# Block products for the Fourier chunks too, a new order of the seven products, and two conditioning groups on TensorE

## The chip, the cores and the metric

The kernel runs on one core of a Trainium2 chip. The metric is the device time of one execution in microseconds, as the median of several runs. A profile is one execution taken by the hardware profiler; its span is the time from the first to the last instruction. Engines: PE is TensorE (matmuls; PEld its weight loads), DVE is VectorE, ACT is ScalarE, POOL is GpSimd, SP issues most of the transfers.

## The reference

Two layers, one after the other, work on 640 tokens (512 latent and 128 context tokens) of width 1024. Of each layer, cut to what matters here:

```python
shift, scale, gate = _modulation(cond, w_mod[l], b_mod[l])        # silu(cond) @ w_mod + b_mod
h = _layernorm(x) * (1.0 + scale) + shift
q, k, v, z_a, cb, cc, cx, z_b, fx, z_c, g = jnp.split(h @ w_in[l], offsets, axis=-1)
y_a = attn_fn(q, k, v) * silu(z_a)
y_b = _short_conv(cb, cc, cx, conv_w[l]) * silu(z_b)
y_c = _fourier(fx) * silu(z_c)          # real part of a 2-D DFT over positions and 128 channels
gates = sigmoid(g.reshape(b, s, 3, 1024))
merged = gates[:, :, 0] * (y_a @ w_branch[l, 0]) + gates[:, :, 1] * (y_b @ w_branch[l, 1]) \
       + gates[:, :, 2] * (y_c @ w_branch[l, 2])
x = _layernorm(ALPHA * x + gate * (merged @ w_o[l])) * ln_g[l] + ln_b[l]
```

## The kernel before

Activations lie with channels on the 128 partitions and the 640 tokens along the free axis. A float32 product is made of three float32r products: each operand is split into a high part (a ScalarE copy) and a low part (a VectorE subtraction), and high·high, high·low and low·high are summed in PSUM. The activations h lie split in the tile `act`.

The input projection of a layer is 58 chunks of 128 columns: Q 4, K 1, V 1, ZA 4, CB, CC, CX and ZB 4 each (the convolution), FX 4 and ZC 4 (the Fourier branch), and 24 of gates. A **plain chunk** (`inproj`, L505 to L507) takes eight k steps of six matmuls (three of 256 and three of 384 tokens), with two split weight buffers `hlw`, one for each half. A **pair** (`pair`, L957) makes two gate chunks at once: it cuts the 2x2 blocks of input halves and chunks so that seven products of 12 matmuls with 320 columns are enough where eight are due. It needs sums of blocks of the activations (tiles `tb` and `tf`, made by `sums(0)`, `sums(1)` and `last_sum` in the Fourier stage) and of the weights (the `Sum` steps), and each product adds to one of three PSUM banks `y`, `x`, `z`, from which ScalarE copies (`keep`) and VectorE adds (`plus`) gather the gate tiles (`ga` for branch 0, `gs` for the others).

The stages of a layer are: LayerNorm and Q, K, V; attention, with the plain ZA and convolution chunks as fillers between its units; the Fourier stage, which alternates plain FX and ZC chunks with `channels(g)` (the DFT over channels) and `positions(g)` (over positions) of four groups; the gate stage, twelve pairs in the order of branches 1, 2, 0, each pair of branch 1 and 2 followed by its two branch products (`pb`); and the output product with the closing LayerNorm.

The program is a list of jobs. `run()` walks through it and puts the weight loads (at most N_RAW = 6 raw buffers) and their splits (at most N_HL = 5 split buffers `hl`) as far ahead of the products as these buffers allow. A scheduler then fixes one order for each engine; on the chip an engine works its list in that order and waits on semaphores. The scratch tiles `tmp` share three buffers: `channels` takes two for its results `ah` and `al`, and the conditioning work takes others.

Conditioning (scale, shift and gate from `w_mod`) comes in groups (l, n). Those of layer 0 that the first LayerNorm needs are made by TensorE at the start (`mod_rows`, L459, and `mod_columns`, L468). The others are made by VectorE: an accumulator `moda` takes 16 operations a group over loads `rawm` (L236 and L239), then a transpose, a reduction and a small matmul. Groups (0,4), (0,5) and (1,0) run as `mod_steps` beside layer 0's attention, the others as `mod_piece`, one after each pair: twelve pieces in layer 0 and eight in layer 1.

## Time and profile before

| | |
|---|---|
| time, median of 3 runs | 1243.19 us (1242.01 to 1244.68) |
| profiled execution of before | 1243.65 us, span 1241.9 us, mean granted clock 0.996 |
| busy: PE, DVE, ACT, POOL | 1211.6, 918.7, 568.3, 182.1 us |
| moved by DMA | 137.38 MB, mean 111 GB/s |

The profiled execution is 1.75 us longer than its span; that part lies outside the instructions. Busy times of the engines overlap, so they don't add up to the span: an engine with a share near 100% sets the pace, and another one matters where it makes that engine wait. A matmul's duration in a row includes its way through the array; how fast matmuls follow one another is read from the starts.

### The profile page before, as it was taken

What the parts mean: (1) busy time and instruction counts of PE and PEld (TensorE: products, weight loads), DVE (VectorE), ACT (ScalarE), POOL (GpSimd) and SP (SyncE); (2) the same over time, 40 slices, a digit from 0 to 9 for tenths busy, and PEclk for the clock granted to TensorE, in tenths of its full rate; (3) what the DMA queues carried; (4) which work ended last, traced back from release to release, by engine and by line L of the source; (5) the groups of instructions that cost most, each with busy time, mean ns of one, the idle gap of its engine ahead of it and who ended that gap; (6) DMA issues with size and microseconds to landing.
All of it is one profiled execution on the core that took longest, in us unless ns stands there. A gap on an engine that the chain in (4) does not pass through costs nothing.

```text
span 1241.9 us, 20937 instructions
## 1 busy us (share of the span) xinstructions
PE 1211.6 (98%) x8016; PEld 1166.8 (94%) x8016; DVE 918.7 (74%) x1683; ACT 568.3 (46%) x1100; POOL 182.1 (15%) x180
## 2 busy tenths in 40 slices
PE   5999999999999999999999999999999999999997
PEld 4899999999999999999889999999999999999986
DVE  5795697879799876677888665666869966666766
ACT  4345636456344344463245646545444344445300
POOL 2003424041000000000230324232000000000001
PEclk8999999999999999999999999999999999999999
DMA  9632131313255452453412211112223533433351
GB/s 353 235 113 69 52 119 60 102 60 120 62 160 153 128 151 71 102 174 135 158 72 82 73 56 60 51 55 93 92 57 125 160 111 92 131 88 106 105 187 51
DMA packets 64085, 137.38 MB, mean 111 GB/s; under 512 B 7600, under 2 KB 8176, under 8 KB 63728
## 3 DMA queue, kind: packets, MB, share of 16 engines
q1 hardware_dynamic: 59232, 125.35, 30.5%
q0 software_dynamic: 4176, 10.39, 4.1%
q8 instruction: 63, 1.03, 0.4%
q10 hardware_dynamic: 576, 0.30, 0.1%
q14 instruction: 38, 0.31, 0.1%
HBM read 130.48 MB, written 5.52 MB: 110 GB/s over the span
## 4 chain that ended last, share of the span: by engine, by line
PE 88%; DVE 6%; DMA 2%; issue 2%; ACT 1%; POOL 1%; DVEq 0%; SPq 0%; POOLq 0%
PE y L957 13%; PE p L505 12%; PE p L507 12%; PE p L506 12%; PE z L957 6%; PE pb L505 4%; PE pb L507 4%; PE pb L506 4%; PE x L957 3%; PE pt L694 2%; PE s L645 2%; PE p L422 2%; PE o L1118 2%; PE o L1117 2%; PE o L1119 2%
## 5 line engine op out<-in xcount | busy, mean ns | idle before, releaser
L505 PE MATMUL p<-act,hlw 128*128 128x256 f32 (+1 forms) x1024 | 321.0, 314 | 0.9 <-ACT qr L69 0.9
L507 PE MATMUL p<-act,hlw 128*128 128x256 f32 (+1 forms) x1024 | 318.9, 311 | 0.0
L506 PE MATMUL p<-act,hlw 128*128 128x256 f32 (+1 forms) x1024 | 317.4, 310 | 0.0
L505 PEld LDWEIGHTS p<-act,hlw 128*128 128x128 f32 x1024 | 193.3, 189 | 2.8 <-ACT qr L69 1.2
L506 PEld LDWEIGHTS p<-act,hlw 128*128 128x128 f32 x1024 | 192.8, 188 | 1.5
L507 PEld LDWEIGHTS p<-act,hlw 128*128 128x128 f32 x1024 | 192.8, 188 | 1.3
L676 POOL TENSOR_SCALAR P<-P,rc 128x384 f32<-128x384 f32 (+2 forms) x80 | 115.5, 1459 | 233.2 <-ACT hlw L69 101.4
L69 ACT ACTIVATE hlw<-raww 128x512 fp32r<-128x512 f32 x136 | 85.2, 629 | 109.0 <-PE p L507 97.0
L147 DVE TENSOR_TENSOR hlw<-raww,hlw 128x512 fp32r<-128x512 f32 x134 | 92.4, 693 | 25.0 <-ACT hlw L69 23.9
L1117 PE MATMUL o<-wo,act 128*128 128x512 f32 (+1 forms) x168 | 63.8, 381 | 0.0
L1118 PE MATMUL o<-wo,act 128*128 128x512 f32 (+1 forms) x168 | 63.5, 379 | 0.0
L1119 PE MATMUL o<-wo,act 128*128 128x512 f32 (+1 forms) x168 | 63.1, 379 | 0.0
L72 DVE TENSOR_TENSOR pT<-pt,pT 128x512 fp32r<-128x512 f32 x60 | 40.1, 685 | 20.9 <-ACT pT L69 20.8
L69 ACT ACTIVATE gs<-y 128x320 f32<-128x320 f32 x48 | 20.8, 433 | 67.3 <-PE y L957 66.3
L239 DVE SCALAR_TENSOR_TENSOR moda<-rawm,scond,moda 128x512 f32<-128x512 f32 x70 | 51.0, 742 | 0.0
L69 ACT ACTIVATE pT<-pt 128x512 fp32r<-128x512 f32 x60 | 34.9, 592 | 31.5 <-PE pt L694 25.0
L648 DVE CUSTOM_DVE_ANT_0 P<-s,mask 128x384 f32<-128x384 f32 (+1 forms) x64 | 38.5, 617 | 10.3 <-PE s L645 10.2
L670 ACT ACTIVATE P<-P,nm 128x384 f32<-128x384 f32 (+1 forms) x64 | 42.1, 658 | 1.2 <-DVE es L72 0.7
L75 DVE TENSOR_TENSOR gs<-pb,gs 128x640 f32<-128x640 f32 x16 | 13.2, 825 | 38.6 <-PE pb L507 38.6
L505 PE MATMUL pb<-ya,hlb 128*128 128x256 f32 (+1 forms) x128 | 40.1, 313 | 0.1
L505 PE MATMUL pb<-yc,hlb 128*128 128x256 f32 (+1 forms) x128 | 39.9, 311 | 0.0
L505 PE MATMUL pb<-yb,hlb 128*128 128x256 f32 (+1 forms) x128 | 39.8, 311 | 0.0
(722 smaller groups left out, 2888.5 us busy)
## 6 DMA issues: line engine op xcount, KB each, us to landing
raww<-in_w_in SPq DMA_DIRECT2D x136, 256.0 KB, 2.9
rawm<-in_w_mod SPq DMA_DIRECT2D x36, 512.0 KB, 4.3
rawg<-in_w_in SPq DMA_DIRECT2D x72, 256.0 KB, 3.4
rawb<-in_w_branch SPq DMA_DIRECT2D x48, 256.0 KB, 3.1
rawo<-in_w_o SPq DMA_DIRECT2D x32, 256.0 KB, 3.0
sz<-in_w_mod SPq DMA_DIRECT2D x24, 256.0 KB, 3.0
dft<-in_dft POOLq DMA_DIRECT2D x2, 1542.0 KB, 7.6
x<-in_x SPq DMA_DIRECT2D x5, 512.0 KB, 8.3
```

The costliest lines, as they stand in the source:

```text
L69: nc.scalar.activation(out, in_, AF.Copy)
L147: eng.tensor_tensor(out=self.hl[:, 1], in0=raw, in1=fr(self.hl[:, 0]), op=ALU.subtract)
L239: nc.vector.scalar_tensor_tensor(out=acc[:, c], in0=w, scalar=scond[:, k, c:c + 1], in1=acc[:, c], op0=ALU.mult, op1=ALU.add)
L505: nc.tensor.matmul(ps[:, a:b], lhsT=ld.w(0, k), rhs=mh, start=k == 0, stop=False)
L506: nc.tensor.matmul(ps[:, a:b], lhsT=ld.w(0, k), rhs=ml, start=False, stop=False)
L507: nc.tensor.matmul(ps[:, a:b], lhsT=ld.w(1, k), rhs=mh, start=False, stop=k == nk - 1)
L670: nc.scalar.activation(P[:, g, :W], srcs[g], AF.Exp, scale=0.125, bias=nm_[:, g:g + 1], accum_out=sm[:, g:g + 1])
L676: nc.gpsimd.tensor_scalar(out=P[:, g, :W], in0=P[:, g, :W], scalar1=rc[:, g:g + 1], scalar2=None, op0=ALU.mult)
L957: nc.tensor.matmul(out, lhsT=ld.w(z, k), rhs=moving(k, y), start=first and k == i == 0, stop=k == 3 and i == 2, skip_group_check=True)
L1117: nc.tensor.matmul(ps, lhsT=act[:, t, 0, k], rhs=w[:, 0], start=k == 0, stop=False)
L1118: nc.tensor.matmul(ps, lhsT=act[:, t, 0, k], rhs=w[:, 1], start=False, stop=False)
L1119: nc.tensor.matmul(ps, lhsT=act[:, t, 1, k], rhs=w[:, 0], start=False, stop=k == NK - 1)
```

## The change

FX and ZC chunks become four pairs per layer, named f{l}0, f{l}2 (FX) and f{l}4, f{l}6 (ZC); their results lie in a tile `fz`. The convolution and ZA chunks stay plain. The block sums move into the attention (`aside` and `last_sum`). The seven products of every pair come in another order of banks, with the weight steps in the order that goes with it. Groups (0,4) and (0,5) are made by TensorE in layer 0's attention (`mod_group`), from loads into tiles of the tags T and F; group (1,0) becomes four more pieces of layer 0's gate stage, sixteen in all, and a pair of branch 2 is followed by two pieces. yb and ya stay unsplit in the attention, and `split_y` splits them in the gate stage. Tiles of SBUF change their tags accordingly, and so do the loads of w_o.

```diff
-        side = mod_steps(((0, 4), (0, 5), (1, 0)) if l == 0 else (), lambda: S["moda"], lambda: S["modr"])
+        if l == 0:
+            aside = {0: [groups[0][1]], 1: [groups[0][2], groups[1][1]], 2: [groups[1][2]]}
+        else:
+            aside = {}
+        aside.update({3: [begin_sums, sums(0)], 6: [sums(1)]})
...
+    def mod_group(l, n, tag):
...
+        def rows():
+            pr = aux(f"modp{l}{n}")
+            for k in range(NK):
+                c = 32 * (k % 4)
+                nc.tensor.matmul(pr[c:c + 32], lhsT=scond32[:, k], rhs=w["raw"][:, k * 512:(k + 1) * 512],
+                                 start=k < 4, stop=k >= 4, tile_position=(0, c))
+            w["rows"] = row(f"modr{l}{n}")[:, 0:512]
+            copy(w["rows"], pr)
+
+        def columns():
+            ps = aux(f"modq{l}{n}")
+            for i in range(4):
+                nc.tensor.matmul(ps[:, 2 * i:2 * i + 2], lhsT=w["rows"][:, i * 128:(i + 1) * 128], rhs=pick,
+                                 start=True, stop=True)
...
-            for i in range(2):
-                mod_add(mod_acc[l, n], 2 * kp + i, mod_raw[p][:, i * 512:(i + 1) * 512])
+            with tc.issue_after(last["gate"].ins):
+                mod_add(mod_acc[l, n], 2 * kp, mod_raw[p][:, 0:512])
+            mod_add(mod_acc[l, n], 2 * kp + 1, mod_raw[p][:, 512:1024])
...
-            job(seventh("y", old(0, 0), True, keep(0, 0)), Load([s1, a11, a12, a22], [hl(a11, [], 1)]))
-            job(seventh("x", old(0, 1), True, plus(0, 0)), Load([], [hl(a12, [], 2)]))
-            job(seventh("z", new(0), True, lambda out: None), Load([], [hl(s1, [], 5), Sum(add, s1, s1, a11)]))
...
-            job(seventh("y", new(1), False, keep(0, 1)), Load([], [hl(s1, [], 6), Sum(sub, a11, s1, a22), Sum(add, a12, a12, s1, [s1])]))
-            job(seventh("y", new(2), False, third_y), Load([], [hl(a11, [a11], 7)]))
-            job(seventh("y", lambda k, z: act[:, :, z, k, 64:128], False, last_y), Load([], [hl(a22, [a22], 4)]))
...
-            job(seventh("z", old(1, 1), False, last_z), Load([], [hl(a12, [a12], 3)]))
+                self.steps = [
+                    (Load([s1, a11, a12, a22], [hl(a11, [], 1)]), "y", old(0, 0), self.keep(0, 0)),
+                    (Load([], [hl(s1, [], 5)]), "z", new(0), self.keep(1, 1)),
+                    (Load([], [Sum(add, s1, s1, a11), hl(s1, [], 6)]), "y", new(1), self.keep(0, 1)),
+                    (Load([], [hl(a12, [], 2)]), "x", old(0, 1), self.plus(0, 0)),
+                    (Load([], [Sum(sub, a11, s1, a22), Sum(add, a12, a12, s1, [s1]), hl(a11, [a11], 7)]), "y", new(2),
+                     self.plus(1, 1)),
+                    (Load([], [hl(a12, [a12], 3)]), "z", old(1, 1), self.last_z),
+                    (Load([], [hl(a22, [a22], 4)]), "y", lambda k, z: act[:, :, z, k, 64:128], self.last_y)]
...
-        inproj(l, C_FX, use_fx(0))
...
-        for g in range(4):
-            job(channels(g))
-            inproj(l, C_ZC + g, use_zc(g))
...
+        p = fourier_pair(C_FX, 0, use_fx)
+        p.emit()
+        p = fourier_pair(C_ZC, 4, use_zc)
+        p.emit(4)
+        job(channels(0))
+        p.emit(2)
+        job(channels(1))
+        p.emit(1)
+        p = fourier_pair(C_FX, 2, use_fx)
+        p.emit(2)
+        job(positions(0))
+        p.emit(3)
+        job(positions(1))
+        p.emit(2)
+        p = fourier_pair(C_ZC, 6, use_zc)
+        p.emit(3)
+        job(channels(2))
+        p.emit(2)
+        job(channels(3))
+        p.emit(2)
+        job(positions(2))
+        job(positions(3))
+
+        pieces = [(1, n, kp) for n in (range(4) if l == 0 else (4, 5)) for kp in range(4)]
...
+                if (b, m) == (1, 0):
+                    job(split_y("yb", "C"))
                 piece()
+                if b == 2:
+                    piece()
+                if (b, m) == (0, 1):
+                    job(split_y("ya", "A"))
+                if (b, m) in ((0, 2), (0, 3)):
+                    load_wo(1, "D", m - 2)
```

On TensorE, at the start of layer 0's gate stage, the list of before reads as follows (`hlg010p` are the split weights of branch 1's first pair, `hlg011p` of its second; what stands ahead of the arrow is the bank):

```order
L957 MATMUL y_3753<-act,hlg010p_3503 128x320 x12
L957 MATMUL x_3774<-act,hlg010p_3583 128x320 x12
L957 MATMUL z_3793<-tb_3030,hlg010p_3586 128x320 x12
L957 MATMUL y_3753<-tb_3030,hlg010p_3697 128x320 x12
L957 MATMUL y_3893<-act,hlg011p_3806 128x320 x2
L957 MATMUL x_3914<-act,hlg011p_3822 128x320 x2
L957 MATMUL y_3753<-tf_3031,hlg010p_3704 128x320 x12
L957 MATMUL y_3893<-act,hlg011p_3806 128x320 x10
L957 MATMUL x_3914<-act,hlg011p_3822 128x320 x10
L957 MATMUL y_3753<-act,hlg010p_3769 128x320 x12
```

The list of the change at the same place:

```order
L825 MATMUL y_3694<-act,hlg010p_3505 128x320 x12
L825 MATMUL z_3715<-tb_1835,hlg010p_3547 128x320 x12
L825 MATMUL x_3750<-act,hlg010p_3603 128x320 x9
L825 MATMUL y_3694<-tb_1835,hlg010p_3564 128x320 x12
L825 MATMUL x_3750<-act,hlg010p_3603 128x320 x3
L825 MATMUL z_3715<-act,hlg010p_3710 128x320 x12
L825 MATMUL y_3694<-tf_1836,hlg010p_3629 128x320 x12
L825 MATMUL y_3843<-act,hlg011p_3747 128x320 x2
L825 MATMUL z_3864<-tb_1835,hlg011p_3764 128x320 x2
L825 MATMUL y_3843<-act,hlg011p_3747 128x320 x10
L825 MATMUL z_3864<-tb_1835,hlg011p_3764 128x320 x10
L825 MATMUL y_3694<-act,hlg010p_3729 128x320 x12
```

The banks of one pair now alternate between y, z and x, the second pair's first two products (y and z instead of y and x) begin ahead of the first pair's last one, and no product on a bank stands directly behind another on the same bank of that pair.

On VectorE at the same place, before (`td`, `te` and `act` are the last block sum, `fy` the Fourier result, `sgzc` the ZC path, `rawg` weight sums):

```order
L147 TENSOR_TENSOR hlg010p_3704<-rawg_3313,hlg010p_3704 128x512
L905 SCALAR_TENSOR_TENSOR td_3709<-te_3710,td_3709 128x640
L236 TENSOR_SCALAR moda_3884<-rawm_3885,scond 128x512 x2
L905 SCALAR_TENSOR_TENSOR td_3716<-te_3717,td_3716 128x640
L147 TENSOR_TENSOR hlg010p_3769<-rawg_3400,hlg010p_3769 128x512
L239 SCALAR_TENSOR_TENSOR moda_3884<-rawm_3885,scond,moda_3884 128x512 x2
L72 TENSOR_TENSOR act<-td_3709,act 128x5x2x64
L78 TENSOR_TENSOR fy_3743<-g_3724,fy_3743 128x256
L72 TENSOR_TENSOR fy_3743<-fy_3743,g_3724 128x255
L875 SCALAR_TENSOR_TENSOR fy_3743<-g_3724,fy_3743 128x128
L147 TENSOR_TENSOR hlg010p_3788<-rawg_3318,hlg010p_3788 128x512
L72 TENSOR_TENSOR act<-td_3716,act 128x5x2x64
```

VectorE with the change, from the split of the fourth product on (`fz` are the Fourier and ZC results):

```order
L147 TENSOR_TENSOR hlg010p_3603<-rawg_3416,hlg010p_3603 128x512
L236 TENSOR_SCALAR moda_3834<-rawm_3835,scond 128x512 x2
L75 TENSOR_TENSOR fz_2924<-fz_2924,sg_3623 128x640
L78 TENSOR_TENSOR rawg_3416<-rawg_3416,rawg010s 128x512
L239 SCALAR_TENSOR_TENSOR moda_3834<-rawm_3835,scond,moda_3834 128x512 x2
L239 SCALAR_TENSOR_TENSOR moda_3834<-rawm_3837,scond,moda_3834 128x512 x2
L147 TENSOR_TENSOR hlg010p_3629<-rawg_3286,hlg010p_3629 128x512
L239 SCALAR_TENSOR_TENSOR moda_3834<-rawm_3837,scond,moda_3834 128x512
L75 TENSOR_TENSOR fz_2924<-fz_2924,sg_3626 128x640
L239 SCALAR_TENSOR_TENSOR moda_3834<-rawm_3837,scond,moda_3834 128x512
```

The block sums are gone from here; the first operations on the accumulator, which belong to group (1,0), stand six ahead of the split `hlg010p_3629` and two behind it, between the second results of the ZC pair.

## Rows read from the trace of the kernel before

**Rows 1.** The page, part 1: busy time of each engine (share of the span), instructions

```profile
PE 1211.6 (98%) x8016; PEld 1166.8 (94%) x8016; DVE 918.7 (74%) x1683; ACT 568.3 (46%) x1100; POOL 182.1 (15%) x180
```

**Rows 2.** Windows: stretch, its length, busy PE, PEld, DVE, ACT, POOL, clock, DMA

```profile
264.00:339.00 75.00, 75.00 (x521) 73.44 (x520) 63.52 (x118) 41.37 (x80) 8.95 (x15) 1.00 0.27 82
339.00:420.00 81.00, 78.85 (x533) 77.72 (x532) 78.35 (x132) 34.73 (x67) 3.46 (x4) 1.00 0.51 153
420.00:505.00 85.00, 84.05 (x570) 83.47 (x569) 56.48 (x93) 35.59 (x68) 4.33 (x5) 1.00 0.42 118
940.00:1020.00 80.00, 77.85 (x526) 76.70 (x526) 71.09 (x118) 34.77 (x67) 3.42 (x4) 1.00 0.46 132
1020.00:1105.00 85.00, 84.94 (x579) 84.62 (x577) 51.89 (x86) 35.07 (x66) 4.07 (x5) 1.00 0.41 115
```

**Rows 3.** Waits of PE, 335 to 610 us: total, times, longest

```profile
PE y L957 <- ACT gs L69: 1.6, 3, 0.5
```

**Rows 4.** Waits of PE, 52 to 335 us

```profile
PE p L505 <- ACT qr L69: 0.9, 1, 0.9
```

**Rows 5.** Timeline of PE: start, duration; two first matmuls of plain k steps, four apart

```profile
54.62 0.28 PE L505 MATMUL p<-act,hlw 128*128 128x256 f32 x1
...
58.16 0.28 PE L505 MATMUL p<-act,hlw 128*128 128x256 f32 x1
```

**Rows 6.** Timeline of PE: gate products of layer 0

```profile
345.07 1.92 PE L957 MATMUL y<-tb,hlg010p 128*128 128x320 f32 x12
346.83 0.46 PE L957 MATMUL y<-act,hlg011p 128*128 128x320 f32 x2
348.25 0.53 PE L957 MATMUL x<-act,hlg011p 128*128 128x320 f32 x2 [0.96 <-DVE gs L78]
...
362.78 1.63 PE L957 MATMUL y<-tb,hlg011p 128*128 128x320 f32 x10
364.94 2.03 PE L957 MATMUL y<-tf,hlg011p 128*128 128x320 f32 x12 [0.53 <-ACT gs L69]
```

**Rows 7.** Timeline of PE, start-up: one conditioning block on TensorE

```profile
30.28 1.07 PE L459 MATMUL modp<-rawm,scond 128*32 128x256 f32 x16
31.28 0.61 PE L468 MATMUL modq<-pick,modr 128*128 128x2 f32 x4
```

**Rows 8.** Timeline of PE: the last positions step, then the first gate product

```profile
336.86 0.28 PE L858 MATMUL g<-dft,ah 128*128 128x258 f32 x1
...
339.33 0.95 PE L957 MATMUL y<-act,hlg010p 128*128 128x320 f32 x5
```

**Rows 9.** Groups by shape of DVE, 264 to 420 us: count, busy us, mean ns

```profile
L239 DVE SCALAR_TENSOR_TENSOR moda<-rawm,scond,moda 128x512 f32<-128x512 f32 x42 | 30.6, 741 | 0.0
...
L75 DVE TENSOR_TENSOR mg<-pb,gs 128x640 f32<-128x640 f32 x6 | 4.9, 818 | 2.5 <-PE pb L507 2.5
...
L78 DVE TENSOR_TENSOR gs<-z,gs 128x320 f32<-128x320 f32 x8 | 3.8, 481 | 0.0
...
L72 DVE TENSOR_TENSOR al<-f,ah 128x256 fp32r<-128x256 f32 x8 | 3.3, 414 | 0.0
...
L236 DVE TENSOR_SCALAR moda<-rawm,scond 128x512 f32<-128x512 f32 x6 | 2.6, 480 | 0.0
L244 DVE STREAM_TRANSPOSE modf<-moda 128x1024 f32<-128x1024 f32 x2 | 2.5, 1234 | 0.0
```

**Rows 10.** Timeline of DVE: first gate split, and two conditioning ops in a row

```profile
319.10 0.68 DVE L147 TENSOR_TENSOR hlg010p<-rawg,hlg010p 128x512 fp32r<-128x512 f32 x1
...
342.70 1.41 DVE L239 SCALAR_TENSOR_TENSOR moda<-rawm,scond,moda 128x512 f32<-128x512 f32 x2
```

**Rows 11.** Timeline of SP: issues of conditioning loads

```profile
328.53 0.33 SPq L287 DMA_DIRECT2D rawm<-in_w_mod  x1
...
339.47 0.33 SPq L287 DMA_DIRECT2D rawm<-in_w_mod  x1
```

**Rows 12.** The page, part 6: KB of each transfer, median us to landing

```profile
rawm<-in_w_mod SPq DMA_DIRECT2D x36, 512.0 KB, 4.3
```

503 lines of the change are left out of this document (256 added, 247 removed).

## The prediction

> **What bounds the kernel now.** I read the page first. TensorE is busy for 98% of the span, VectorE for 74% [rows 1], so TensorE sets the end, and a microsecond of its work or of its waiting is a microsecond of the time wherever nothing stands behind it. The windows by stage say where that breaks. In the Fourier stage of layer 0 (264 to 339 us) TensorE is never idle and VectorE has 63.5 of 75 us. Right after it, where the gate products begin (339 to 420), TensorE loses 2.15 us and VectorE is at 78.35 of 81 us; in the next stretch VectorE falls to 56 of 85. Layer 1 repeats this (940 to 1105), with the granted clock at its upper level throughout [rows 2]. So the start of each gate stage is the one place where both engines are full, and it is what I price most carefully. The waits of TensorE name the rest: three of 0.5 us on a ScalarE copy of the bank y, because three products in a row write y [rows 3], and one of 0.9 us in layer 0's Q chunks, on a copy that is late while VectorE and ScalarE serve the conditioning work beside the attention [rows 4]. Readers should note that a wait costs more than the idle time shown. The product on y that began again at 362.78 with ten matmuls at 1.76/12 us each would have ended at 364.25; the next starts at 364.94, so 0.69 us are lost where 0.53 are shown [rows 6].
>
> **The change, part by part.**
>
> *Chunks to pairs.* Four k steps of a plain chunk take 3.54 us from first matmul to first matmul [rows 5], a chunk of eight 7.08, two 14.16. One block product takes 346.83 − 345.07 = 1.76 us [rows 6], seven 12.32. A pair saves 1.84 us, and the eight pairs (four per layer) 14.7 us of TensorE. No reason is in sight why a product in the Fourier stage should run otherwise than in the gate stage: same shape, same operands' kind.
>
> *Conditioning groups on TensorE.* The row step of a start-up block (eight matmuls of 256 columns) takes 31.28 − 30.28 = 1.0 us and its column step 0.6 [rows 7]. A new group has 512 columns and twice the column matmuls: 2.0 + 1.0 us, an estimate by doubling the rows, and two groups +6.0 us. They stand in the attention, where TensorE has no gap to hide them in. A page of the Trainium skill would price them lower: TensorEngine Tiling (Array Packing), Tiling Modes, says that tiles work independently and can load and multiply in parallel, with up to four times the speed where a side is 32 wide. The eight matmuls show as sixteen records of 0.0625 us each, while a chunk's 24 matmuls of 320 columns on average take 0.148 us each [rows 5], 0.118 for 256 columns: a factor of two and not four. By the page the two groups would cost 2 us less and the sum would be that much lower. I keep the row. What VectorE gains in the attention by losing these groups buys nothing but the 0.9 us wait of [rows 4], which I take as gone: −0.9.
>
> *Order of the seven products.* y, z, y, x, y, z, y never writes a bank twice in a row within a pair, so the waits on the copy of y should go. In the four full stretches of the gate stages TensorE's idle time is 2.15, 0.95, 2.15 and 0.06 us, 5.3 in all [rows 2]; with 0.16 us hidden behind each wait and the delayed weight loads, some of it outside these windows, I put the loss at 9 (5.3 is the lower bound, twice that the upper). Gone: −9.
>
> *The start of the gate stage.* Here I see the gain going back. A split (one ScalarE copy, one VectorE subtraction) can be issued only into one of five buffers, so it is at most five products ahead. While a plain chunk takes 3.5 us per split, five buffers are a long lead: in the kernel before, the first gate split is done at 319.8 and its product starts at 339.33, a lead of 19.5 us [rows 8, 10]. After the change the products before the gates last 1.76 us. In the new order, when the buffer of the first gate split comes free, TensorE still has four products of f06 (7.0 us) and the channels and positions steps of groups 2 and 3 ahead. A positions step takes 339.33 − 336.86 = 2.47 us [rows 8]; a channels step has half as many matmuls, about 1.2 as an estimate; together 7.3. From the 14.3 us go 1.6 for the copy, the 0.68 us subtraction [rows 10] and the hand-over: the lead is 12.7 us.
>
> From there to the split of product 3 of pair 011 the VectorE order lists 64 instructions: 14 moda accumulations at 0.741 and two scalings at 0.480 (conditioning pieces, which the scheduler put this early, before the gate of the first pair is done), 14 splits and sums of weights at 0.68, 11 of 640 columns at 0.818 (the Fourier remainder and the split of yb that used to lie in the attention), 6 of 320 at 0.481, 16 of 128 to 384 at about 0.414, and a transpose of 1.234 [rows 9, 10]. That is 10.4 + 1.0 + 9.5 + 9.0 + 2.9 + 6.6 + 1.2 = 40.6 us. Two moda in a row take 1.41 us and not 1.48 [rows 9, 10], so each instruction overlaps its neighbour by about 0.075: 4.8 us come off, 35.8 stay. In this time TensorE has nine products to do, 15.8 us. 35.8 − 15.8 − 12.7 = 7.3 us are missing, and TensorE waits for them. Before, the same place had 19.5 us of lead and still ended with a wait of 0.96 us [rows 6]. Layer 1 has nearly the same order and the same count of pieces. I take 7 us per layer, +14. Afterwards the pairs have 12.3 us of products against less VectorE work, and the lag is not exceeded again.
>
> *The Fourier stage itself.* TensorE's work there falls by 7.4 us per layer while VectorE's stays about what it was (the block sums move to the attention, the weight sums and adds of the pairs come in): 63.5 us in what becomes 67.6 [rows 2]. This works only if nothing in VectorE's order waits, and it waits there for each product's result. Bounds 0 to 3 us per layer; I take 1.5, as the stage stays below the 97% at which the gates' start lost time: +3.
>
> *At nothing:* the block sums and the undone splits in the attention lie beside TensorE work there (if VectorE were full, each 0.82 us would count); the wo loads only change tiles; issue_after around the first accumulation of a piece moves nothing in the listed order.
>
> The sum: −14.7 + 6.0 − 0.9 − 9.0 + 14.0 + 3.0 = −1.6 us. The profiled execution took 1243.65 us, with 1.75 us outside its span; the runs' median is 1243.19, 0.46 lower, and 1.6 off the median gives 1241.6 us.
>
> **The rivals.**
>
> *A, VectorE keeps up:* the pieces' operations are held back by late loads or the order is better than my count, and neither stage start waits. For it speaks VectorE's 74% over the whole span [rows 1]; against it that 64 listed instructions are there in a fixed order and the windows already show 97% in the like place. Then −14.7 + 6.0 − 0.9 − 9.0 + 2 for small waits = −16.6: 1226.6 us.
>
> *B, slower: VectorE stands still in front of a late conditioning load.* Loads and accumulators share three buffers with the Fourier step's intermediates. Before, the first load was issued at 328.53, but the second only at 339.47, when the last positions step had let its buffer go [rows 8, 11]; a load lands after 4.3 us [rows 12]. In the new order the first moda stands ahead of three more splits of pair 010, and everything behind it on VectorE waits with it. If its load is issued only after positions(2), it lands about 4 us after VectorE gets there, and the lag grows from 7 to 11 us per layer; with the Fourier stage at its upper bound of 3, the sum is −1.6 + 8 + 3 = +9.4: 1252.6 us. It decides from the point where the load lands later than VectorE reaches its first use. Against it: group 0's buffer is free long before, so one load can go early, as it did. The Trainium skill (TensorE: Matmul & The Clock Gate, the table at its head) has VectorE's queue as strictly first in, first out, eight deep; by that rule nothing behind a waiting moda can pass it, and in this trace VectorE's instructions do start in the listed order.
>
> *C, the new bank order changes nothing* because the waits of y come back as waits on z or on the splits: 4.5 of the 9 us stay, 1246 us.
>
> **How the numbers follow.** The likeliest case (0.5) has the VectorE-bound start of the gates at 5 to 9 us per layer and the time between 1236 and 1246. A has 0.2 (1223 to 1232), B 0.2 (1246 to 1256), C 0.1 (1243 to 1248). The range 1228 to 1251 leaves out a good half of A and the upper half of B, some 2 in 10. A measurement can tell about 0.2%, 2.5 us, from no change: the bounds are 1240.7 and 1245.7. Faster: A and not quite half of the likeliest case, 0.43; same: 0.3; slower: B and the rest of C, 0.27.
>
> **What would show it.** Right: the Fourier stage's TensorE work shorter by 7 us per layer, no wait of y for ScalarE in the gates, and instead waits of 5 to 9 us in sum at each gate stage's start, on copies and subtractions of hlg010p to hlg012p, with VectorE above 95% there and moda between the splits. Wrong: VectorE idle there (A, or B if its idle time ends on rawm), waits inside the Fourier stage of more than 3 us per layer, or a conditioning group that takes TensorE longer than 3 us or waits for its load.

## The result: 0.56% slower, and the profile after

The changed kernel takes 1249.89 us (median of 4 runs, 1248.86 to 1251.4); the kernel before takes 1242.87 in the same comparison. The ratio is 1.0056, 95% interval 1.0038 to 1.0073: slower, where the forecast of 1241.6 was a hair faster. By these medians the change costs 7.0 us. The profiled execution, the slowest of the four, took 1251.4 us with a span of 1249.6. In its trace TensorE's upper clock level is shown as 0.95, not 1.00, but products follow each other every 1.76 us as before (352.66 − 350.90 below), so only falls to 0.50 count.

The page of the changed kernel, part 1, answers to [rows 1]: TensorE is busy as long as before in a span that is 7.7 us longer.

```profile
PE 1212.0 (97%) x7964; PEld 1161.5 (93%) x7964; DVE 931.2 (75%) x1711; ACT 586.5 (47%) x1148; POOL 196.3 (16%) x188
```

The windows, shifted to the same stages as in [rows 2] (columns as there; the clock is the third from the end):

```profile
265.00:342.00 77.00, 73.83 (x509) 71.61 (x507) 66.19 (x124) 41.75 (x84) 9.10 (x13) 0.95 0.38 110
342.00:423.00 81.00, 78.37 (x504) 77.03 (x504) 79.52 (x134) 35.66 (x71) 2.56 (x3) 0.91 0.51 153
423.00:508.00 85.00, 85.00 (x582) 85.00 (x581) 63.20 (x107) 34.87 (x66) 4.29 (x5) 0.95 0.41 116
946.00:1026.00 80.00, 77.68 (x502) 76.73 (x503) 68.63 (x113) 36.08 (x71) 2.58 (x3) 0.91 0.41 119
```

Three things are to be seen beside [rows 2]. TensorE now idles 3.2 us in the first of these stretches, where it idled not at all; 1.7 of them are the gap ahead of the first gate product, shown below. At the gates' start of layer 0 VectorE has 79.5 of 81 us, fuller than before. In layer 1 it has only 68.6 of 80, but in the first 22 us of the stage it is as full there as in layer 0:

```profile
946.00:968.00 22.00, 19.68 (x116) 18.73 (x117) 21.89 (x38) 12.45 (x27) 0.00 (x0) 0.87 0.32 99
```

And the clock column is below its level where the gates begin, in both layers; before, it was at 1.00 in all these rows.

**Where the 7.7 us went.** I cut both traces at starts of matmuls: the first score product of each layer, the first gate product, the first output product. For each stretch I also add up the loss: what the distances between matmul starts exceed the usual distance of their shape (the median in the trace of before).

| stretch | before | after | difference |
|---|---|---|---|
| start to first score, layer 0 | 83.00 | 81.76 | −1.24 |
| to first gate product (attention, Fourier) | 256.33 | 260.47 | +4.14 |
| to first output product (gates) | 221.62 | 222.96 | +1.34 |
| to first score, layer 1 (the layer boundary) | 123.62 | 127.92 | +4.30 |
| to first gate product, layer 1 | 255.91 | 253.10 | −2.81 |
| to first output product | 220.84 | 222.61 | +1.77 |
| rest | 80.6 | 80.8 | +0.2 |

| loss in us | before | after |
|---|---|---|
| Fourier stage with the step to the first gate product, layers 0 and 1 | 1.45, 1.44 | 5.79, 5.76 |
| gates, layers 0 and 1 | 5.41, 4.86 | 6.53, 6.62 |
| layer boundary | 1.24 | 5.54 |

The waits of TensorE over the whole span (total, times, longest) name the new places. None is a wait of `y` for the copy of `gs` any more, as in [rows 3]; the wait of [rows 4] is gone too.

```profile
PE y L825 <- ACT fy L69: 3.9, 2, 1.9
PE y L825 <- ACT hlg011p L69: 1.5, 1, 1.5
PE yzf L825 <- ACT fz L69: 1.5, 4, 0.5
PE f L949 <- DVE a L72: 1.4, 2, 0.7
PE y L825 <- ACT hlg111p L69: 1.3, 1, 1.3
```

**The gates' start.** The timeline of TensorE in the changed kernel, first gate products of layer 0 (start, duration, idle time and its releaser); it answers to [rows 6]:

```profile
342.23 2.94 PE L825 MATMUL y<-act,hlg010p 128*128 128x320 f32 x12 [1.93 <-ACT fy L69]
344.97 2.57 PE L825 MATMUL z<-tb,hlg010p 128*128 128x320 f32 x12
347.38 1.48 PE L825 MATMUL x<-act,hlg010p 128*128 128x320 f32 x9
...
350.90 1.92 PE L825 MATMUL z<-act,hlg010p 128*128 128x320 f32 x12
352.66 1.92 PE L825 MATMUL y<-tf,hlg010p 128*128 128x320 f32 x12
...
361.41 0.55 PE L825 MATMUL y<-tb,hlg011p 128*128 128x320 f32 x2 [1.55 <-ACT hlg011p L69]
...
363.27 2.86 PE L825 MATMUL y<-tb,hlg011p 128*128 128x320 f32 x10 [0.27 <-DVE hlg011p L147]
```

There are two gaps. The first product waits 1.93 us for a PSUM bank that holds a result of the last positions steps. ScalarE has to copy it out, and its own list (timeline of ScalarE, same kernel) has a weight copy and a sigmoid of the ZC path in front:

```profile
340.39 0.62 ACT L69 ACTIVATE hlg010p<-rawg 128x512 fp32r<-128x512 f32 x1
340.91 0.73 ACT L773 ACTIVATE sg<-fz 128x640 f32<-128x640 f32 x1
341.53 0.65 ACT L69 ACTIVATE fy<-g 128x257 f32<-128x257 f32 x2
```

The second gap is the one that was forecast: the splits of hlg011p are late. On VectorE the conditioning pieces stand among the splits, from 336.25 us on (timeline of VectorE, same kernel):

```profile
338.38 2.74 DVE L239 SCALAR_TENSOR_TENSOR moda<-rawm,scond,moda 128x512 f32<-128x512 f32 x4
341.04 0.69 DVE L147 TENSOR_TENSOR hlg010p<-rawg,hlg010p 128x512 fp32r<-128x512 f32 x1
```

Behind each gap the products are slow. The windows of the same kernel, one microsecond each, show why:

```profile
343.00:344.00 1.00, 1.00 (x6) 1.00 (x5) 1.00 (x3) 0.06 (x1) 0.00 (x0) 0.50 0.57 215
...
364.00:365.00 1.00, 1.00 (x5) 1.00 (x5) 1.00 (x2) 0.00 (x0) 0.00 (x0) 0.50 0.73 295
```

The granted clock is 0.50, the lower of its two levels (1.2 GHz), for some 3.4 us, though TensorE is busy. From 342.23 to 347.38 run 24 matmuls that take 2 × 1.76 = 3.52 us at the upper level; they took 5.15, so these products end 1.6 us later. There are five such stretches behind gaps: at 343, 363, 612, 947 and 967 us. Five times 1.6 would be 8 us, as much as the whole slowdown; but whether the 1.6 us are lost depends on what stands behind the products, and at the gates' start they were not (e11). Before, there is no such stretch between the start-up and the last products.

**The layer boundary.** The timeline of VectorE at the end of layer 0's gates, before:

```profile
584.60 0.83 DVE L72 TENSOR_TENSOR act<-mg,act 128x640 fp32r<-128x640 f32 x1 [0.81 <-ACT act L69]
585.34 2.49 DVE L72 TENSOR_TENSOR wo<-rawo,wo 128x512 fp32r<-128x512 f32 x4
...
593.44 0.69 DVE L1133 SCALAR_TENSOR_TENSOR xr<-xr,oy 128x512 f32<-128x512 f32 x1 [1.93 <-DMA xr<-in_x]
```

and after:

```profile
588.47 1.89 DVE L72 TENSOR_TENSOR wo<-rawo,wo 128x512 fp32r<-128x512 f32 x3
590.27 0.68 DVE L147 TENSOR_TENSOR hlw<-raww,hlw 128x512 fp32r<-128x512 f32 x1
590.88 0.82 DVE L72 TENSOR_TENSOR act<-mg,act 128x640 fp32r<-128x640 f32 x1
...
601.65 1.29 DVE L1202 SCALAR_TENSOR_TENSOR xr<-xr,oy 128x512 f32<-128x512 f32 x2 [1.40 <-DMA xr<-in_x]
```

The splits of the last quarter of w_o have moved ahead of the last split of `mg`. This quarter has the tile with the tag A in both kernels; what lies there ahead of it has changed. Before, it is `ga`, which the last merge on VectorE reads; now it is the split of ya (`sya`), which the last branch product on TensorE reads, and ScalarE's copies for w_o begin as soon as that product is done (timeline of ScalarE, after):

```profile
586.39 2.19 ACT L69 ACTIVATE wo<-rawo 128x512 fp32r<-128x512 f32 x4 [0.95 <-PE pb L512]
```

The residual rows `xr` are loaded into mg's tile, so their load is issued behind the split of `mg`, and the residual sum, the LayerNorm and the transposes `tr` of layer 1 follow. After the change (timeline of SP, then of TensorE):

```profile
592.76 3.94 SPq L1145 DMA_DIRECT2D xr<-in_x  x4
```

```profile
612.54 1.77 PE L319 MATMUL tr<-ident,xn 128*128 128x128 f32 x8 [2.14 <-ACT xn L303]
```

Before, the load went at 585.45 and the first `tr` at 605.89 waited for nothing. Now there is a gap of 2.14 us, and a lower-clock stretch behind it.

### The profile page after: what moved, and what is told of

Same layout as the page of the kernel before. It is cut to its first block, busy times and chain, and to the rows that moved or that the text cites. A ratio compares the mean times of both kernels' runs of the same rounds, so it can differ in the third digit from the quotient of the medians.

```text
span 1249.6 us, 20917 instructions
## 1 busy us (share of the span) xinstructions
PE 1212.0 (97%) x7964; PEld 1161.5 (93%) x7964; DVE 931.2 (75%) x1711; ACT 586.5 (47%) x1148; POOL 196.3 (16%) x188
## 4 chain that ended last, share of the span: by engine, by line
PE 84%; DVE 8%; DMA 3%; issue 2%; ACT 1%; POOL 1%; SPq 0%; DVEq 0%; POOLq 0%; ACTq 0%
PE y L825 12%; PE p L510 9%; PE p L512 9%; PE p L511 9%; PE z L825 6%; PE yzf L825 5%; PE pb L510 4%; PE pb L512 4%; PE pb L511 4%; PE x L825 3%; PE o L1186 2%; PE o L1187 2%; PE o L1188 2%; PE pt L701 2%; PE s L652 2%; DMA rawm<-in_w_mod 2%
## 5 line engine op out<-in xcount | busy, mean ns | idle before, releaser
L510 PE MATMUL p<-act,hlw 128*128 128x256 f32 (+1 forms) x768 | 241.2, 314 | 0.0
L511 PE MATMUL p<-act,hlw 128*128 128x256 f32 (+1 forms) x768 | 238.7, 311 | 0.0
L512 PE MATMUL p<-act,hlw 128*128 128x256 f32 (+1 forms) x768 | 238.7, 311 | 0.0
L683 POOL TENSOR_SCALAR P<-P,rc 128x384 f32<-128x384 f32 (+2 forms) x80 | 119.4, 1507 | 195.2 <-DVE rc L681 82.4
L510 PEld LDWEIGHTS p<-act,hlw 128*128 128x128 f32 x768 | 145.1, 189 | 2.3 <-issue 0.9
L512 PEld LDWEIGHTS p<-act,hlw 128*128 128x128 f32 x768 | 144.6, 188 | 1.5
L511 PEld LDWEIGHTS p<-act,hlw 128*128 128x128 f32 x768 | 144.6, 188 | 1.2
L69 ACT ACTIVATE hlw<-raww 128x512 fp32r<-128x512 f32 x104 | 65.0, 629 | 75.2 <-PE p L512 61.3
L147 DVE TENSOR_TENSOR hlw<-raww,hlw 128x512 fp32r<-128x512 f32 x102 | 71.1, 700 | 26.3 <-ACT hlw L69 25.2
L239 DVE SCALAR_TENSOR_TENSOR moda<-rawm,scond,moda 128x512 f32<-128x512 f32 x84 | 60.9, 743 | 1.4 <-DMA rawm<-in_w_mod 1.4
L147 DVE TENSOR_TENSOR hlb<-rawb,hlb 128x512 fp32r<-128x512 f32 x48 | 32.9, 685 | 28.5 <-ACT hlb L69 28.5
L78 DVE TENSOR_TENSOR sm<-sm,es 128x4 f32<-128x4 f32 x20 | 3.2, 162 | 51.6 <-ACT P L677 51.6
L510 PE MATMUL pb<-syb,hlb 128*128 128x256 f32 (+1 forms) x128 | 40.4, 315 | 0.0
L512 PE MATMUL pb<-syb,hlb 128*128 128x256 f32 (+1 forms) x128 | 40.0, 312 | 0.0
L510 PE MATMUL pb<-sya,hlb 128*128 128x256 f32 (+1 forms) x128 | 39.9, 312 | 0.0
```

The source lines that it names most:

```text
L69: nc.scalar.activation(out, in_, AF.Copy)
L147: eng.tensor_tensor(out=self.hl[:, 1], in0=raw, in1=fr(self.hl[:, 0]), op=ALU.subtract)
L239: nc.vector.scalar_tensor_tensor(out=acc[:, c], in0=w, scalar=scond[:, k, c:c + 1], in1=acc[:, c], op0=ALU.mult, op1=ALU.add)
L510: nc.tensor.matmul(ps[:, a:b], lhsT=ld.w(0, k), rhs=mh, start=k == 0, stop=False)
L511: nc.tensor.matmul(ps[:, a:b], lhsT=ld.w(0, k), rhs=ml, start=False, stop=False)
L512: nc.tensor.matmul(ps[:, a:b], lhsT=ld.w(1, k), rhs=mh, start=False, stop=k == nk - 1)
```

## The experiments

The theories: **V**, VectorE is in arrears at the gates' start because the conditioning pieces (`moda`) stand in its list ahead of the splits. **S**, the loss there comes from ScalarE's copies and the bank alone. **W**, the boundary's loss comes from the w_o splits ahead of the last merged split. Every kernel is compared with the kernel before, which took 1242.4 to 1243.1 us in each comparison.

| run | median us | ratio, 95% interval |
|---|---|---|
| e1_hold_pieces | 1268.83 | 1.0220 (1.0207 to 1.0233) |
| e2_positions_apart | 1251.30 | 1.0067 (1.0055 to 1.0079) |
| e3_wo3_behind | 1245.26 | 1.0022 (1.0013 to 1.0031) |
| e4_old_order | 1253.07 | 1.0076 (1.0062 to 1.0089) |
| e5_hold_fold_later | 1238.93 | 0.9971 (0.9958 to 0.9984) |
| e6_fill_gap | 1246.32 | 1.0028 (1.0019 to 1.0038) |
| e7_plain_fourier | 1265.78 | 1.0186 (1.0172 to 1.0199) |
| e8_no_groups | 1239.25 | 0.9968 (0.9956 to 0.9981) |
| e9_hold_x_early | 1238.34 | 0.9966 (0.9954 to 0.9979) |
| e10_all | 1237.72 | 0.9964 (0.9950 to 0.9978) |
| e11_late_pieces | 1244.27 | 1.0018 (1.0009 to 1.0026) |
| e12_rows_behind_x | 1231.55 | 0.9916 (0.9903 to 0.9930) |

**e1: hold the pieces back.** In the change, `last["gate"]` names a ScalarE sigmoid, and the listed order on VectorE has moda ahead of the gate. Here it names a VectorE addition of the same pair.

```diff
...
             def last_z(self, out):
-                self.plus(0, 1)(out)
+                last["gate"] = nc.vector.tensor_tensor(out=quarter(self.G[0], 1), in0=out, in1=quarter(self.G[0], 1),
+                                                       op=ALU.add)
```

> The changed kernel, with the conditioning pieces really held behind their pair: the instruction that issue_after names is now VectorE's last addition of the pair and not a ScalarE sigmoid, so on VectorE no moda operation can stand ahead of it. Theory V (VectorE's list is too full at the start of the gate stage, and each gap of TensorE there is followed by some 3.4 us at the lower clock): the waits on hlg011p, hlg111p and hlg012p and the second stretch at the lower clock in each layer go away, 1.7 + 1.7 + 1.0 us in layer 0 and about as much in layer 1, so about 8 us less than the change: 1241 to 1243. The first gap (first gate product behind ScalarE's fy copies) stays. Rival S (the copies of ScalarE, not VectorE, are late): the same waits stay, 1248 to 1251.

Neither came: 1268.83. The waits on the splits of the second and third pair and the second lower-clock stretch are gone in both layers, as V says. But the pieces end later, and TensorE stands at the small `fold` product that sums a group, with everything queued behind it (waits of TensorE):

```profile
PE modq L250 <- DVE modg L246: 16.0, 3, 5.4
```

So the edge cures the gates' start and starves another wait. That had to be mended before V could be priced.

**e2: the last two positions steps apart.** With them back to back, their four bank results and the gate's `y` want the banks at once.

```diff
-        p.emit(2)
-        job(channels(3))
-        p.emit(2)
+        p.emit(4)
         job(positions(2))
+        job(channels(3))
         job(positions(3))
```

> The changed kernel, with all seven products of pair f6 ahead of the last two positions steps, and channels(3) between these: positions(2), channels(3), positions(3) instead of channels(3), two products, positions(2), positions(3). Theory P (the first gate product waits for a PSUM bank, because two positions steps in a row hold all four and ScalarE copies them out only after the ZC sigmoids): the 1.9 us wait on fy and the stretch at the lower clock behind it go away in both layers, 2.0 + 1.7 us each, 1242 to 1244. Rival V (VectorE is behind anyway, so the bank is only the first to be named): the gap moves to the splits of hlg010p or hlg011p and little is won, 1247 to 1250.

The wait on `fy` went, and nothing was won. The waits of TensorE (in a trace of 1247.55 us, the fastest of its five executions) show the time at the second gap, which grew from 1.5 and 1.3 to 2.7 us:

```profile
PE y L825 <- ACT hlg011p L69: 2.7, 1, 2.7
PE y L825 <- ACT hlg111p L69: 2.7, 1, 2.7
```

S fails as the whole story: TensorE arrives earlier at the place where VectorE is late.

**e3: the last w_o splits behind the last merged split.**

```diff
...
-                    split(w[:, 0, 2 * q + z], w[:, 1, 2 * q + z], ld.raw(z))
+                    with tc.issue_after(last["merged"].ins) if i == 3 else ExitStack():
+                        split(w[:, 0, 2 * q + z], w[:, 1, 2 * q + z], ld.raw(z))
```

> The changed kernel, with the four VectorE splits of the last w_o tile held behind the split of the last merged chunk, as they stood before the change. Theory W (in the change they stand ahead of it, because their tile comes free earlier; the residual's load, which overwrites the merged tile, then starts later, and so do the LayerNorm and the first transpose of layer 1): the wait of about 2.1 us for xn at the layer boundary and the 3.4 us at the lower clock behind it go away, 4 us less: 1245 to 1246.5. Rival D (the residual's load is late because of the other loads in the queue): no change, 1249 to 1251.

1245.26, 4.6 us below the change. The boundary's loss falls from 5.54 to 1.96 us, `tr` waits 0.18 us, and the clock stays up there. W is shown: the place of these splits made the boundary's loss. That they moved because of what lies in their tile is read from the kernel and from ScalarE's row above; no run put the tiles back. The kernels e6, e7, e8 and e11 start from this one.

**e4: the old order of the gate pairs' products** (y, x, z, y, y, y, z), with the rest of the change.

```diff
+                if old_order:
...
+                        (Load([], [hl(a12, [], 2)]), "x", old(0, 1), self.plus(0, 0)),
+                        (Load([], [hl(s1, [], 5), Sum(add, s1, s1, a11)]), "z", new(0), lambda out: None),
```

> The changed kernel, with the gate pairs in the old order of products y, x, z, y, y, y, z; the Fourier pairs keep the new one. Theory O (the order was worth what the waits of before on y show): the waits of y for ScalarE's copy come back, four or five of 0.7 us per layer, 5 to 8 us more than the change: 1255 to 1258. Rival: at the start of the gate stage VectorE sets the pace in either order and the old one hides its waits there; 1 to 3 us more, 1251 to 1253.

1253.07: the order is worth some 3 us here (the two intervals overlap), not the 9 of the sum. The gates' loss rises from 6.53 to 9.99 us in layer 0 and not at all in layer 1 (6.62 and 6.58). The waits of y for gs and ga are back (6.2 us in all), but while TensorE stands at them VectorE catches up, and the wait on hlg011p shrinks to 0.3 us. The two terms of the forecast, −9 for the order and +14 for VectorE, are not independent: waits on one hide waits on the other.

**e5: e1 and e3 together, and the fold product later.** The fold product of a group becomes a job of its own behind the next pair.

```diff
+        pending.append((l, n, part))
+
+    def mod_fold():
...
         ps2 = aux(f"modq{l}{n}")
-        nc.tensor.matmul(ps2[:, 0:32], lhsT=fold, rhs=part.rearrange("p s j a -> p (s j a)"), start=True, stop=True)
+        with tc.issue_after(last["mm"].ins):
+            nc.tensor.matmul(ps2[:, 0:32], lhsT=fold, rhs=part.rearrange("p s j a -> p (s j a)"), start=True, stop=True)
...
                 before = (b, m, y) if b else None
+                job(mod_fold)
```

> The changed kernel with the last w_o splits held behind the merged chunk (1245.3 us so far), the conditioning pieces held behind their pair on VectorE, and the small matmul that closes a conditioning group put behind the products of the next pair on TensorE, so that TensorE doesn't stand at it as it did when only the pieces were held. Theory V (the pieces ahead of the splits are what makes the gate stage's start late): the second gap of each layer and its stretch at the lower clock go away, 3.5 to 4 us per layer: 1237 to 1239. Rival: the VectorE work that is put off makes another wait further on, 1243 to 1247.

1238.93, faster than both kernels. In VectorE's timeline the first moda now starts at 352.15, behind the pair's addition on `gs`, instead of standing among the first splits:

```profile
351.75 0.48 DVE L1052 TENSOR_TENSOR gs<-z,gs 128x320 f32<-128x320 f32 x1
352.15 0.87 DVE L236 TENSOR_SCALAR moda<-rawm,scond 128x512 f32<-128x512 f32 x2
```

The gates' loss falls to 0.26 and 0.86 us, from 6.5 and 6.6. V is shown: the pieces' place in VectorE's list made the arrears. Layer 1 shows it best beside e3: the bank gap there is the same in both, no lower clock follows it in either, and the loss falls from 6.42 to 0.86. The later fold product has no part in this, since the change has no wait for it. One thing is unexpected. The bank wait is still there, and of the same size, but no slow product follows it (timeline of TensorE):

```profile
340.58 2.03 PE L834 MATMUL y<-act,hlg010p 128*128 128x320 f32 x12 [1.93 <-ACT fy L69]
342.45 1.92 PE L834 MATMUL z<-tb,hlg010p 128*128 128x320 f32 x12
```

The boundary, on the other hand, lost 6.25 us again: TensorE came earlier, and the residual load did not.

**e6: keep TensorE busy in the first gap.** e3 with eight extra matmuls between the last positions step and the first gate product.

```diff
+        def fill_gap():
+            d = mmt(f"fill{l}")
+            with tc.issue_after(behind["pos"].ins):
+                for k in range(NK):
+                    nc.tensor.matmul(d[:, 0:320], lhsT=trig[:, 0, 0], rhs=act[:, :, 0, k, 0:64], start=k == 0,
+                                     stop=k == NK - 1)
+        job(fill_gap)
```

> The changed kernel with the last w_o splits held behind the merged chunk (1245.3 us so far), and eight extra matmuls of 320 columns (1.2 us, into a PSUM tile that nothing reads) on TensorE between the last positions step and the first gate product, where it is idle for 1.9 us. Theory C (the stretch at the lower clock behind the gap costs 1.7 us by itself): the idle time there is under 1 us, the clock stays at its upper level, 3.4 us less in both layers, 1242. Theory L (VectorE's list sets when the second pair's third product can start, so what TensorE wins ahead of it is waited for there): the clock stays up at the first gap, the wait at hlg011p grows by as much, and the time stays at 1245 to 1246.

1246.32, a hair above theory L's times. No lower clock follows the first gap now (in e3 one followed it in layer 0 only), and the time is not better than e3's. TensorE arrives at the second gap earlier, waits 1.9 and 2.0 us for the subtractions of hlg011p and hlg111p, and the clock falls there (windows, layer 0):

```profile
361.00:362.00 1.00, 0.12 (x1) 0.12 (x1) 1.00 (x3) 0.00 (x0) 0.00 (x0) 0.50 0.00 0
362.00:363.00 1.00, 1.00 (x4) 1.00 (x5) 1.00 (x3) 0.00 (x0) 0.00 (x0) 0.50 0.74 176
```

But the lower clock was only moved: between the start-up and the last products e3's trace has 10.2 us of it, and so has e6's. What a better clock alone would buy as long as VectorE sets the pace, this run doesn't show; e11 does.

**e7: the Fourier chunks plain again,** in e3. These chunks read the block of `act` that the last block sum has already replaced, so this kernel computes other Fourier results; it is run for its times.

```diff
-        p = fourier_pair(C_FX, 0, use_fx)
-        p.emit()
...
+        plain_fx(0)
+        plain_fx(1)
+        for g in range(4):
+            job(channels(g))
+            plain_zc(g)
+            job(positions(g))
```

> The changed kernel with the last w_o splits held behind the merged chunk (1245.3 us so far), and the eight FX and ZC chunks of each layer plain again, with the channels and positions steps in the order of the kernel before; all other parts of the change stay. Theory G (what the pairs save on TensorE is given back because VectorE's lead at the gates is gone, and the steps of the Fourier stage wait): TensorE's work grows by 14.7 us, and the waits of the Fourier stage and the gates' start fall by 7 to 9 us per layer: 1241 to 1246. Rival A (the waits come from the conditioning pieces alone, lead or no lead): 1256 to 1260.

1265.78, above the times of both theories. TensorE's Fourier work grows by 7.24 us per layer, which is the saving by pairs as forecast. Some of the rest is this kernel's own: its chunks wait for the block sum (waits of TensorE):

```profile
PE p L510 <- ACT act L69: 7.3, 2, 3.7
PE p L511 <- DVE act L72: 4.4, 2, 2.2
```

With slow products ahead of them and so a long lead, the gates still lose 5.34 and 5.04 us (6.30 and 6.42 in e3). That speaks against my account by the lead of 12.7 us: the lead matters little, the pieces' place much. Because of the extra waits this is support for V, not proof.

**e8: without the two groups on TensorE,** in e3; a constant stands in place of groups (0,4) and (0,5).

```diff
         def rows():
-            pr = aux(f"modp{l}{n}")
...
+            pass
```

> The changed kernel with the last w_o splits held behind the merged chunk (1245.3 us so far), without the two conditioning groups (0,4) and (0,5): neither their loads nor their matmuls are there, a constant stands in their place, so layer 0's output gate is wrong. If the two groups cost TensorE 6 us, as forecast by doubling the start-up blocks: 1239.3. If the trace of the change is right, where the attention stage carries 7 us for them: 1238.3. Rival (they lie in gaps): 1244 to 1246.

1239.25, 6.0 us below e3, as the term of the sum has it. In the trace layer 0's attention is 7.0 us shorter (163.92 for 170.96), and the boundary loses 1 us more than in e3.

**e9: the residual rows earlier.** e5 with `xr` in the tile of `ga`, which is free before mg's, and the rows (gates, ln_g, ln_b) in mg's; and ScalarE's copies of the last w_o quarter behind its last merged copy.

```diff
-            S["xr"] = big.tile([128, NT, 1024], F32, name=f"xr{l}", tag="B")
-            rowt = big.tile([128, 5120], F32, name=f"rows{l}", tag="C")
+            S["xr"] = big.tile([128, NT, 1024], F32, name=f"xr{l}", tag="C")
+            rowt = big.tile([128, 5120], F32, name=f"rows{l}", tag="B")
```

> Like e5_hold_fold_later, with two edits at the layer boundary: the residual xr takes the tile that ga leaves (tag C) instead of the one that mg leaves, and the rows take mg's; and the ScalarE copies of the last w_o splits stand behind the copy of the last merged chunk. Theory W (the boundary loss hangs on the residual load: in e5 it is issued at 584.86, behind the last merged split, lands only at 593.9 beside 2 MB of row loads, and the transposes of layer 1 stand 2.9 us with a lower clock behind them): the load is issued at about 582, lands some 3 us earlier, the wait of tr goes, and the time is 1234 to 1236, 3 to 5 us below e5's 1238.93. Rival: the rows (the gate's row first) now land late instead and the first product of oy waits for them: 1238 to 1240.

1238.34: the rival. Now the gate's row is late, behind four residual loads (timeline of VectorE):

```profile
592.91 1.89 DVE L75 TENSOR_TENSOR oy<-o,rows 128x512 f32<-128x512 f32 x3 [5.74 <-DMA rows<-gates]
```

In this stretch the transfers are themselves the limit: from 583 to 593 us the DMA engines are 91% busy. What matters is which load goes first.

**e10: e9 with e2's edit.**

> Like e9_hold_x_early, and the last two positions steps stand apart as in e2_positions_apart. With VectorE in arrears (e2) the gap only moved. Theory V (the arrears come from the conditioning pieces, which are held back here): the bank wait of 2.0 us per layer goes and nothing takes its place: 3 to 4 us below e9, 1230 to 1232. Rival (VectorE's lead is short even without the pieces): the wait comes back on the copies or subtractions of hlg010p or hlg011p, and the time is within 1 us of e9.

1237.72, not to be told from e9. The bank wait shrinks from 1.9 to 1.1 us in each layer, and 0.9 us stand at the positions step instead (`g` for the subtraction of `a`): the loss up to the first gate product falls only from 5.73 to 5.10 us, and the boundary, which TensorE reaches earlier, takes 1.2 us back (5.12 to 6.34). Neither theory had that.

**e11: no pieces behind the first two pairs,** in e3, without an edge.

```diff
-                piece()
-                if b == 2:
+                if (b, m) not in ((1, 0), (1, 1)):
+                    piece()
+                if b == 2 or l == 0 and b == 0 and m < 2:
                     piece()
```

> Like e3_wo3_behind, with no conditioning piece behind the first two gate pairs of a layer; layer 0 makes up for them with two pieces behind pairs 000 and 001, layer 1 ends its eight in branch 2 anyway. No edge is added. Theory V (the pieces on VectorE are what the gate's start is short of): the waits for hlg011p and its second lower-clock stretch go, the bank wait of 2.0 us may stay; 3 to 5 us per layer less than e3's 1245.26, so 1236 to 1240. Rival (the shorter lead of the products themselves is the cause): waits on hlg010p and hlg011p stay, above 1243.

1244.27, 1 us below e3 and not to be told from it, and no test of V: the scheduler put the operations where they were before. VectorE's timeline has the first moda ahead of the gates (334.71 in e3):

```profile
335.08 0.88 DVE L236 TENSOR_SCALAR moda<-rawm,scond 128x512 f32<-128x512 f32 x2
```

Where a job stands in the program is not where its instructions stand in the list; only an edge on the right engine moved them.

But this trace settles what the lower clock costs at the gates' start. The bank gap and the gap at hlg011p are there in both layers, of the same length. In layer 0 no lower clock follows, in layer 1 two stretches of it do (windows of the first 23 us of gates):

```profile
341.00:364.00 23.00, 20.07 (x127) 18.63 (x128) 23.00 (x39) 12.98 (x28) 0.00 (x0) 1.00 0.31 108
940.00:963.00 23.00, 20.99 (x120) 19.98 (x121) 23.00 (x39) 12.94 (x27) 0.00 (x0) 0.88 0.30 110
```

The gates lose 6.1 us in layer 0 and 6.3 in layer 1. VectorE is busy for all of the 23 us in both, and without the lower clock TensorE stands longer at late splits and results: 3.7 us of waits behind the first product in layer 0, 2.3 in layer 1. The change and e3 agree: with e11 these are six layers, with 0, 3.4 or 6.8 us at the lower clock at the gates' start, and they lose 6.1 to 6.6 us, whichever it is. So there the pace is VectorE's, and the slow products hide behind it.

**e12: the order of the loads.** e10 with the tiles of e5 again; the ln rows and the second gate row are issued behind the first two residual loads.

```diff
-            nc.sync.dma_start(out=rows[:, 2], in_=I["ln_g"][l].partition_broadcast(128))
-            nc.sync.dma_start(out=rows[:, 3], in_=I["ln_b"][l].partition_broadcast(128))
-            gates(1)
+            with tc.issue_after(last["x"].ins):
+                nc.sync.dma_start(out=rows[:, 2], in_=I["ln_g"][l].partition_broadcast(128))
+                nc.sync.dma_start(out=rows[:, 3], in_=I["ln_b"][l].partition_broadcast(128))
+                gates(1)
```

> Like e10_all, but xr and the rows have their tiles of e5_hold_fold_later again, and of the loads at the layer boundary only the row of the gate stands ahead of the first two residual loads; the rows of ln_g and ln_b and the second gate row are issued behind them. In e5 the residual load was issued at 584.86 behind 2 MB of rows and landed 9 us later; in e9_hold_x_early it went first and the gate's row came as late (592.9). Theory D (the boundary waits for the order of 4 MB that all go at some 400 GB/s, not for a tile): with 1.5 MB instead of 2.5 ahead of it, the first residual load lands at 588 to 590, the wait of tr (2.9 us, and the lower clock behind it) goes, and the time is 1232 to 1235. Rival (the layer boundary is bound by VectorE's own chain of residual, moments and norm): the load lands earlier and tr waits as long: 1237 to 1238.

1231.55 us: 0.84% faster than the kernel before (0.70 to 0.97%) and 18 us below the change. The first residual sum no longer waits (timeline of VectorE; 593.89 in e5):

```profile
588.97 1.28 DVE L1223 SCALAR_TENSOR_TENSOR xr<-xr,oy 128x512 f32<-128x512 f32 x2
```

The boundary's loss is 1.53 us (6.25 in e5, 5.12 in e9, 6.34 in e10; no run has the order of the loads as its only edit), that of the gates nothing in either layer (0.04 and −0.29), and the clock stands at its upper level from the start-up to the last products (windows, 30 to 1225 us):

```profile
30.00:1225.00 1195.00, 1183.60 (x7837) 1141.32 (x7836) 914.83 (x1667) 572.54 (x1123) 189.99 (x172) 1.00 0.35 108
```

## Why the prediction was wrong

The sum was −1.6 us; the trace shows +7.7, the medians +7.0. By its own steps:

- **Chunks to pairs, −14.7.** Right: TensorE's work in the Fourier stage is 7.24 us shorter per layer, 14.5 in all.
- **Conditioning groups, +6.0.** Right: 6.0 by e8, 7.0 by the trace, which is 3.5 a group and above the 3 that I had named as a sign of being wrong. My case against the page of the Trainium skill (TensorEngine Tiling (Array Packing), Tiling Modes) was a misreading, though. The page says that tiles work in parallel, and the trace agrees: of a group's row step in the changed kernel the first four records start within 0.03 us, and no other starts before 112.60 us (windows of `modp`: length, busy PE with the records, clock, DMA).

```profile
112.16:112.19 0.03, 0.02 (x4) 0.95 0.00 0
112.16:112.60 0.44, 0.43 (x4) 0.95 0.34 61
```

The row of the start-up that I doubled had this in it already, so there were no 2 us to take off. I had held float32 records against the float32r products of a chunk; what these matmuls would take without tiles no run shows.

- **The Q wait, −0.9.** Right in that the wait is gone. The stretch is 1.24 us shorter here, but its length differs between executions by more than the term: 79.94 us in e2 and 80.22 in e12, which leave it as it is in the change (81.76).
- **Order of the products, −9, and start of the gate stage, +14.** Both mechanisms are there. All waits of y for the copy of gs are gone, and VectorE is late with hlg011p behind moda. The net was forecast at +5. The gates' losses (6.53 + 6.62, and 2.04 of the first product in each layer) less those of before (10.27) make +7.0. The term of +14 was mis-sized: it is 17.2. VectorE's arrears, which I had counted alone, are some 12 of it: so much goes when the pieces are held back (0.26 and 0.86 are left in e5). What the sum did not have is the bank that ScalarE copies late, 2.04 us per layer. The waits that the trace shows, with the bank, are 4.3 and 4.0 us per layer, less than the 5 to 9 that were to show it. The lower clock behind these gaps is no term of its own (e11). Nor do the two terms add as I wrote them: e4 shows that here the order is worth 3.
- **The Fourier stage, +3.** Mis-sized: the loss there grows by 2.3 us per layer (4.34 and 4.32, less 2.04 for the first gate product), 4.6 in all; that is inside the bounds of 0 to 3 per layer and above the 1.5 that I took. The waits are `yzf` for the copies of fz and `f` for the subtraction of `a`.
- **"At nothing: ... the wo loads only change tiles."** This step failed. Which tile a result is written to decides behind which reader it may be written. With another tenant in tile A the last splits of w_o were free earlier, they slid ahead of the last merged split, and the boundary lost 4.3 us. e3 gives back 4.6 in the time, 3.6 of them at the boundary in its trace.

Summed: −14.5 + 7.0 − 1.2 + 7.0 + 4.6 + 4.3 + 0.2 for the rest is +7.4, beside 7.7 measured. Of the miss of 9.3 us, 4.3 is the boundary, 2.0 the gates, 1.6 the Fourier stage, 1.0 the groups.

Of the rivals, A (VectorE keeps up) was not this kernel, but it is what e5 and e12 made of it by holding the pieces back; the 1226.6 us worked out for A lie 5 below e12. B (a late conditioning load) is seen once, 1.4 us at 375 us, behind the gates' start and not ahead of it; it is not the cause. C was half right: no wait of y came back as one on z, but there are waits on the splits, and by e4 only 3 us of the 9 are won by the order here.

I had read the granted clock in [rows 2] as a constant. Before, the longest gap after the start-up is 1.13 us beyond the usual distance of starts; the five of the change that were followed by the lower clock are 1.47 to 2.30 us long, counted in the same way, and e12's longest is 1.21.

**Still open:** why the lower clock follows some gaps and not others. The bank gap (1.93 us shown, 2.04 counted) stands with the same length in both layers of the change and of e1, e3, e5, e8, e9 and e11, and was followed by it in eight of these fourteen cases; in e3 and e11 in one layer and not in the other. What the new order is worth once the pieces are held back was not run either. What remains in e12 of the Fourier stage's loss, 5.07 us per layer, was not taken further.

## What to carry to other kernels

A tile with another tenant moves whatever is written there next: look where that stands in each engine's list before pricing it at nothing. A wait removed ahead of an engine that is late comes back at its next result, so first relieve the late engine (an edge that names an instruction on that same engine), then the waits, then the order of transfers behind it. Look behind a gap on TensorE for slow products, and price them only where no late engine waits behind them.

## What the runs showed of the hardware

A gap of 1.5 to 2.3 us on TensorE was followed, in the change, by some 3.4 us at half the granted clock, although TensorE was busy again: 24 products took 5.15 us instead of 3.52. It isn't certain: of fourteen gaps of the same length at the same place, six were followed by none. And it isn't always a loss. At the gates' start, with VectorE late, two such stretches cost nothing that can be told (6.3 us of loss with them and 6.1 without, e11). At the layer boundary one costs about its 1.6 us: e6 has a gap of 1.70 us there, no lower clock behind it and a loss of 3.29, e2 a gap of 2.08, a stretch at the lower clock and 5.28.

Four float32 matmul records, on tiles of 32 columns of the array, started within 0.03 us and ran side by side; the next started more than 0.4 us later (the row step of a conditioning group).

Where the transfers fill the DMA engines (0.90 of them busy from 582 to 594 us in e5), a 512 KB load took 9 us from issue to first use, against 4.3 in [rows 12].
